# First layer's norm gain moved from the input into the split of the weights, and 39 unread matmuls at the end

## The chip, the cores and the metric

The kernel runs on one core of a Trainium2 chip. The metric is the device time of one execution in microseconds (us); the median of the runs is compared. The engines are TensorE (PE in the profile; its weight loads, PEld, overlap its matmuls), VectorE (DVE), ScalarE (ACT), GpSimd (POOL) and SyncE (SP), which here only issues DMAs. Every engine takes its instructions in the order in which they were written to its queue. A row of a trace gives the start in us, the duration, the engine, the line of the kernel, the operation, out<-in by the program's names, and in square brackets the idle time before it with what ended it.

## The reference

A trunk of four residual layers over 256 tokens of width 1024, float32: pooling mixer, gated DeltaNet, latent attention, pooling mixer again, and a last norm. Each layer adds `mixer(rmsnorm(x, g))` to `x`. What the change touches is the norm and the first product of the first layer:

```python
def rmsnorm(x, g):
    xf = x.astype(jnp.float32)
    y = xf * lax.rsqrt(jnp.mean(xf * xf, axis=-1, keepdims=True) + EPS)
    return (y * g.astype(jnp.float32)).astype(x.dtype)

def pool_mixer(h, w_in, w_grp, scale, w_out):
    B, S, _ = h.shape
    u, gate = jnp.split(h @ w_in, 2, axis=-1)   # w_in: 1024 x 4096
...
    y = p * scale * jax.nn.silu(gate)
    return y @ w_out
```

The DeltaNet layer inverts, for each of 8 heads and 2 chunks of 128 tokens, a unit lower triangle built from keys; the kernel does that by substitution in 32 x 32 blocks and products of blocks.

## The kernel before

Tokens are two tiles of 128 (t = 0, 1), the width is 8 channel tiles of 128 (k). A float32 product is made of three float32r products: both operands are split into a high and a low part (hi, lo) and hi·hi, hi·lo and lo·hi are summed in PSUM.

- *Weights.* `weights()` loads a unit of one or two channel tiles by 512 columns (`raw`, L104, one DMA of SP's queue, 256 or 512 KB), and splits each channel tile: ACT casts it to `whi` (L117), DVE, or POOL for the tiles listed in `pool`, subtracts that from `raw` to get `wlo` (L119). `whi` and `wlo` lie in rings of 9 slots; a `raw` buffer is free for the next load when both have read it. `project()` runs the products token-major (L167, 512 columns of weights) or channel-major (L127 to L129, 256 tokens).
- *The norm.* `part_done` squares and sums a row's part on ACT (L209); POOL makes the mean and its inverse root `xr` (L245 to L251, L296). `Normed.rest` makes h = x * xr * gain, on DVE (L303); where POOL has already made `hg` = x * gain (L291), ACT scales that (L308). `gain` is the layer's vector, broadcast to 128 partitions by two DMAs of 256 KB (L276). `LayerIn.feed` transposes h on PE (L323) and splits it into `hTh` (ACT, L195) and `hTl` (DVE, L200).
- *The start.* 24 transposes of the identity (L270) run on PE while x and the first weights load. SP's queue asks for x of tile 0, then the gains with the first weights between them, then the second tile's x among more weights. Six units of weights of the first product, gate 3 of layer 0, are prefetched as single tiles.
- *The DeltaNet layer* goes through a written list, `g0 k0 d a0 g1 k1 a1 s q0 v0 i v1 v2 q1 g2 u0 v3 u1 g3`: gates (g), keys (k), triangles (a), the substitution (s), queries (q), values (v), inverses (i). Convolutions of queries and values run on DVE (L636, tiles `cv`, `vc`). The substitution stores triangles (L718), loads them as one row of 32 x 32 blocks (`Lb`, L721), runs 31 steps of two operations each on POOL (`pr` L726, `Tb` L730), stores the result (`d_t`, L732) and loads it into `T` by 8 DMAs (L736), on SP's queue. The inverses begin with DVE's transpose U<-T (L797) and PE's products with T (L806).
- *Order.* The code is not run as written: the framework's scheduler, which works with a timeline of its own, puts the instructions of each engine in an order when the kernel is built, and also chooses the number of buffers where the code gives none. So an edit in layer 0 can change the order in other layers. Positions below are taken from the built programs.
- *The end.* `layer_out` adds the last output product to x in parts (L353), the last norm follows, and two DMAs store each tile (L346).

Of the kernel before, what the change touches and what calls it, by code (L numbers as in the profile page):

```python
# [42 lines left out]
def trunk(ctx: ExitStack, tc: tile.TileContext, x, positions, norm_g, pool_w_in, pool_w_grp,  # L43
# [53 lines left out]
    def weights(src, n, cols, raw=None, pool=()):  # L97
        """One unit of weights, split into two float32r parts that add up to it."""
# [11 lines left out]
        for k in range(n):  # L110
# [5 lines left out]
            with later(*(held_back["after"] if held else ())):  # L116
                a = nc.scalar.copy(hi, v)  # L117
                e = nc.gpsimd if k in pool else nc.vector
                b = e.tensor_tensor(out=lo, in0=v, in1=hi.bitcast(F32), op=ALU.subtract)  # L119
# [11 lines left out]
    def project(src, ks, act, cols=CW, chan=False, tail=0, done=None, cuts=1,  # L131
                where="acc", pool=()):
        """act (channel-major, split) times a block of columns; src(k0, n) is its weights.

        ks lists the units (first channel tile, how many), in the order to go through them.
        Token-major: one bank per token tile; channel-major: one bank per two
        channel tiles. The last `tail` units go by token tile and by `cuts` parts of the columns,
        each followed by done(t, part, its bank).
        """
        first, last = ks[0][0], sum(ks[-1]) - 1  # L140

        def unit(k0, n):
            return weights(src(k0, n), n, cols,
                           pool=[a for a in range(n) if (k0 + a) % KD in pool])
# [16 lines left out]
        def rows(t, c, k0, n, parts):  # L161
            o, sl = banks[t][c][:, :width], slice(c * width, (c + 1) * width)
            for x, y in ((0, 0), (0, 1), (1, 0)) if n == 1 else ((0, None), (1, 0)):
                for j in range(n):
                    k = k0 + j
                    for z in (0, 1) if y is None else (y,):
                        nc.tensor.matmul(o, lhsT=act(k, t * P, P)[x], rhs=parts[j][z][:, sl],  # L167
                                         start=k == first and x == z == 0,
                                         stop=k == last and x == 1)
# [21 lines left out]
    def split_out(*tiles):  # L191
        """Tiles of one bank, each (times a per-partition scale) into two float32r parts."""
# [18 lines left out]
    class Split:  # L211
        """Channel-major activations in two float32r parts, four channel tiles to a tile."""
# [20 lines left out]
    # ---- the residual stream. The square sum of a row but its last part goes along with that  # L233
    # part, as the square of one more column ----
# [23 lines left out]
    load_x(0)  # L258
    neghalf = const.tile([P, 2], F32, name="neghalf")
# [5 lines left out]
    # the activation table and TensorE's clock, while the first loads run  # L265
# [3 lines left out]
    for _ in range(WARM):  # L269
        nc.tensor.transpose(ps[:, :P], ident, ident)  # L270

    def gain_tile(row, between):
        g = gp.tile([P, D], F32, tag="gain", name="gain")
        for c in range(2):
            sl = slice(c * CW, (c + 1) * CW)
            nc.sync.dma_start(out=g[:, sl], in_=row[:, sl].to_broadcast([P, CW]))  # L276
            if c == 0 and between:
                between()
        return g

    class Normed:
        """The residual over its mean square's root, times a gain. Every other part of a row
        meets the gain before the root is known."""

        def __init__(self, row, between=None):
            self.g, self.early = gain_tile(row, between), {}
# [7 lines left out]
        def rest(self, t):  # L294
# [17 lines left out]
    class LayerIn(Normed):  # L312
        """The normed residual of a layer, channel-major, made one token tile at a time."""

        def __init__(self, i, between=None):
            super().__init__(norm_g[i:i + 1, :], between)
            self.hT = Split("hT", KD)
# [30 lines left out]
    def layer_out(w, yT, ks, i):  # L348
        """The output projection into the residual, and the start of the next layer."""
# [5 lines left out]

        project(cols_of(w, 0), ks, yT, done=lambda t, c, ps: done(t, 0, ps))
# [41 lines left out]
    def window_counts():  # L398
        """w / (t + 1) for the first tokens of the pooling windows."""
# [10 lines left out]
    # ================= multi-scale causal pooling =================  # L410
    def pool_layer(i, j, hT):
        yT = Split("yT", POOL_W // P)
        order = (3, 2, 1, 0)

        def gate(g):
            ks = [(k, 1) for k in range(KD)] if g == order[0] and i == 0 else units(KD)
            banks = project(cols_of(pool_w_in[j], POOL_W + g * CW), ks, hT, chan=g != order[0])
# [5 lines left out]
        def pooled(g):  # L423
            w = WINDOWS[g]
            banks = project(cols_of(pool_w_in[j], g * CW), units(KD), hT, chan=True)
# [67 lines left out]
    # ================= gated DeltaNet =================  # L493
    GC = {}

    def gdn_setup():
# [16 lines left out]
        # convolution taps, one column per (tap, channel tile)  # L513
# [21 lines left out]
    def gdn_layer(i, j, hT):  # L535
# [27 lines left out]
        # beta and the log decays  # L563
# [38 lines left out]
        # decays: DT[t][j, h, i] = exp(G_i - G_j) for i >= j, and exp(G_i) for the second chunk  # L602
# [25 lines left out]
        def conv(*tiles):  # L628
            """Causal depthwise convolution of the channel tiles of a bank."""
# [10 lines left out]
        # the substitution's unit diagonals, and room for the inverses  # L640
# [18 lines left out]
        def channels(dst, c0, hf, which):  # L659
            """Four heads of keys or queries, channel-major, and their square sums."""  # L660
# [586 lines left out]
```

## Time and profile before

| | us |
|---|---|
| median of 3 runs | 872.19 (870.34 to 872.74) |
| span of the profiled execution | 864.8 |
| PE busy | 843.5 |
| DVE busy | 590.0 |
| ACT busy | 488.1 |
| POOL busy | 156.6 |

The profiled execution's own time is known as its span, from its first to its last instruction on the engines; the median of the runs is 7.4 us above it. In the page the busy time of each engine is a share of the span, the chain that ended last follows the work back from the last instruction to what released it, and the waits say how long an engine stood idle and what ended that. In the view of windows a row gives a stretch, its length, the busy time of PE, PEld, DVE, ACT and POOL with the count of instructions, then the clock that PE was granted (1.00 is full), the share of the DMA engines' time, and GB/s. In a row of groups, the numbers behind the bar are busy time in us, mean duration in ns, and idle time before with what ended it.

### The profile page before, as it was taken

What the parts mean: (1) busy time and instruction counts of PE and PEld (TensorE: products, weight loads), DVE (VectorE), ACT (ScalarE), POOL (GpSimd) and SP (SyncE); (2) the same over time, 40 slices, a digit from 0 to 9 for tenths busy, and PEclk for the clock granted to TensorE, in tenths of its full rate; (3) what the DMA queues carried; (4) which work ended last, traced back from release to release, by engine and by line L of the source; (5) the groups of instructions that cost most, each with busy time, mean ns of one, the idle gap of its engine ahead of it and who ended that gap; (6) DMA issues with size and microseconds to landing.
All of it is one profiled execution on the core that took longest, in us unless ns stands there. A gap on an engine that the chain in (4) does not pass through costs nothing.

```text
span 864.8 us, 16123 instructions
## 1 busy us (share of the span) xinstructions
PE 843.5 (98%) x5965; PEld 779.9 (90%) x5965; DVE 590.0 (68%) x1138; ACT 488.1 (56%) x1007; POOL 156.6 (18%) x290
## 2 busy tenths in 40 slices
PE   7999999999999979999999999999999999999996
PEld 6999998988999868888989989988978989999986
DVE  5588776466889666466567658767766667867852
ACT  5566655468756535455555645555554566565542
POOL 4010000233258932022202002000000110000012
PEclk8999999999999989999999999999999999999999
DMA  6766656557565463123567676632542547566651
GB/s 211 235 194 185 183 172 219 171 158 228 158 172 168 124 191 102 46 84 137 146 183 221 170 171 194 190 104 75 171 146 59 181 144 207 188 180 191 196 194 50
DMA packets 111288, 140.43 MB, mean 162 GB/s; under 512 B 23340, under 2 KB 53224, under 8 KB 111208
## 3 DMA queue, kind: packets, MB, share of 16 engines
q1 hardware_dynamic: 109056, 138.17, 53.4%
q0 software_dynamic: 320, 1.06, 0.4%
q8 instruction: 47, 0.77, 0.4%
q10 hardware_dynamic: 1832, 0.16, 0.2%
q14 instruction: 33, 0.27, 0.1%
HBM read 137.79 MB, written 1.58 MB: 161 GB/s over the span
## 4 chain that ended last, share of the span: by engine, by line
PE 85%; POOL 7%; DVE 3%; DMA 2%; issue 1%; ACT 1%; SPq 1%; POOLq 0%; ACTq 0%; DVEq 0%
PE acc L167 34%; PE acc L128 11%; PE acc L127 11%; PE acc L129 11%; PE aux L127 2%; POOL Tb L730 2%; PE aux L128 2%; POOL pr L726 2%; PE aux L129 2%; DMA gain<-in_norm_g_dram 1%; PE aux L1134 1%; DVE h L303 1%; DVE wlo L119 1%; PE aux L688 1%; PE tp L1159 1%
## 5 line engine op out<-in xcount | busy, mean ns | idle before, releaser
L119 DVE TENSOR_TENSOR wlo<-raw,whi 128x512 fp32r<-128x512 f32 (+1 forms) x491 | 336.9, 709 | 166.6 <-ACT whi L117 160.1
L117 ACT CAST whi<-raw 128x512 fp32r<-128x512 f32 (+1 forms) x508 | 301.4, 617 | 262.8 <-PE acc L167 92.3
L127 PE MATMUL acc<-hTh,whi 128*128 128x256 f32 x832 | 235.8, 284 | 3.3 <-DVE cv L636 3.3
L128 PE MATMUL acc<-hTl,whi 128*128 128x256 f32 x832 | 236.1, 284 | 0.0
L129 PE MATMUL acc<-hTh,wlo 128*128 128x256 f32 x832 | 235.4, 283 | 0.0
L127 PEld LDWEIGHTS acc<-hTh,whi 128*128 128x128 f32 x832 | 158.2, 190 | 4.2 <-ACT whi L117 3.7
L128 PEld LDWEIGHTS acc<-hTl,whi 128*128 128x128 f32 x832 | 158.3, 190 | 0.4
L129 PEld LDWEIGHTS acc<-hTh,wlo 128*128 128x128 f32 x832 | 158.3, 190 | 0.2
L167 PE MATMUL acc<-whi,yTh 128*128 128x256 f32 (+1 forms) x384 | 116.3, 323 | 0.0
L167 PE MATMUL acc<-wlo,yTh 128*128 128x256 f32 (+1 forms) x384 | 116.2, 319 | 0.0
L167 PE MATMUL acc<-whi,yTl 128*128 128x256 f32 (+1 forms) x384 | 92.4, 321 | 0.0
L167 PEld LDWEIGHTS acc<-whi,yTh 128*128 128x128 f32 x384 | 71.9, 188 | 5.2
L167 PEld LDWEIGHTS acc<-wlo,yTh 128*128 128x128 f32 x384 | 72.0, 188 | 5.1
L167 PEld LDWEIGHTS acc<-whi,yTl 128*128 128x128 f32 x384 | 63.1, 188 | 5.6
L291 POOL TENSOR_TENSOR hg<-x,gain 128x256 f32<-128x256 f32 x18 | 15.4, 860 | 271.7 <-DVE x L353 267.9
L167 PE MATMUL acc<-wlo,hTh 128*128 128x512 f32 (+1 forms) x144 | 56.5, 396 | 0.8 <-DVE wlo L119 0.5
L167 PE MATMUL acc<-whi,hTh 128*128 128x512 f32 (+1 forms) x144 | 55.9, 394 | 0.7 <-ACT hTh L195 0.7
L167 PE MATMUL acc<-whi,hTl 128*128 128x512 f32 (+1 forms) x144 | 45.8, 390 | 0.0
L434 POOL COPY win<-u 128x4 f32<-128x4 f32 x8 | 2.8, 353 | 176.8 <-ACT u L428 176.8
L167 PEld LDWEIGHTS acc<-wlo,hTh 128*128 128x128 f32 x144 | 27.4, 191 | 7.6 <-DVE wlo L119 2.1
L167 PEld LDWEIGHTS acc<-whi,hTh 128*128 128x128 f32 x144 | 27.5, 191 | 6.6 <-ACT hTh L195 1.4
L119 POOL TENSOR_TENSOR wlo<-raw,whi 128x512 fp32r<-128x512 f32 x17 | 23.6, 1389 | 49.4 <-ACT whi L117 49.3
(336 smaller groups left out, 1440.8 us busy)
## 6 DMA issues: line engine op xcount, KB each, us to landing
raw<-in_pool_w_in_dram SPq DMA_DIRECT2D x60, 512.0 KB, 4.5
raw<-in_gdn_w_in_dram SPq DMA_DIRECT2D x48, 512.0 KB, 3.9
raw<-in_pool_w_out_dram SPq DMA_DIRECT2D x32, 512.0 KB, 3.9
raw<-in_mla_w_in_dram SPq DMA_DIRECT2D x24, 512.0 KB, 4.4
raw<-in_mla_w_uq_dram SPq DMA_DIRECT2D x36, 256.0 KB, 3.4
raw<-in_pool_w_grp_dram SPq DMA_DIRECT2D x16, 512.0 KB, 4.0
raw<-in_gdn_w_out_dram SPq DMA_DIRECT2D x16, 512.0 KB, 3.7
raw<-in_mla_w_ukv_dram SPq DMA_DIRECT2D x32, 256.0 KB, 3.2
```

The source lines that it names most:

```text
L117: a = nc.scalar.copy(hi, v)
L119: b = e.tensor_tensor(out=lo, in0=v, in1=hi.bitcast(F32), op=ALU.subtract)
L127: nc.tensor.matmul(o, lhsT=lhs[0], rhs=rhs[0], start=start, stop=False)
L128: nc.tensor.matmul(o, lhsT=lhs[0], rhs=rhs[1], start=False, stop=False)
L129: nc.tensor.matmul(o, lhsT=lhs[1], rhs=rhs[0], start=False, stop=stop)
L167: nc.tensor.matmul(o, lhsT=act(k, t * P, P)[x], rhs=parts[j][z][:, sl], start=k == first and x == z == 0, stop=k == last and x == 1)
L291: nc.gpsimd.tensor_tensor(out=self.early[t, a], in0=xs[t][:, sl], in1=self.g[:, sl], op=ALU.mult)
L303: nc.vector.scalar_tensor_tensor(out=h[:, cut:], in0=xs[t][:, sl], scalar=r[:, 0:1], in1=self.g[:, sl], op0=ALU.mult, op1=ALU.mult)
L688: nc.tensor.matmul(ps[:, b], lhsT=kT[hf][:, b, tt], rhs=rhs[hf][:, b, tt], start=True, stop=True)
L726: nc.gpsimd.tensor_tensor(out=pv, op=ALU.mult, in0=Lb[:, r, r + 1:, None].to_broadcast([M * Q, n, c]), in1=Tb[:, r:r + 1, :c].to_broadcast ...
L730: nc.gpsimd.tensor_tensor(out=tv, in0=tv, in1=pv, op=ALU.subtract)
L1134: nc.tensor.matmul(ps[:, spans[0]], lhsT=r0[bb, pr], rhs=krT[bb], start=False, stop=False)
```

## The change

Layer 0 no longer multiplies its input by the gain; the gain of channel tile k scales the rows of the weights of that tile while they are split. For this the 1024 gains are loaded as 8 rows of 128 (4 KB, ACT's queue, L269 of the changed kernel), transposed on PE in the middle of the 24 warm-up transposes and copied to `gain0`, one column per channel tile (DVE). In the split, ACT's cast becomes an activation with a scale, and the subtraction a scalar_tensor_tensor (raw * gain - whi), always on DVE. h of layer 0 is x * xr, one tensor_scalar. The two broadcast DMAs of layer 0, POOL's two `hg` and its one `wlo` of layer 0 go. Behind the last product 39 matmuls follow, whose results nobody reads. Other layers are computed as before. Comments and docstrings are dropped, which is left out here.

```diff
-    def weights(src, n, cols, raw=None, pool=()):
+    def weights(src, n, cols, raw=None, pool=(), gains=None):
...
-                a = nc.scalar.copy(hi, v)
-                e = nc.gpsimd if k in pool else nc.vector
-                b = e.tensor_tensor(out=lo, in0=v, in1=hi.bitcast(F32), op=ALU.subtract)
+                if gains is not None:
+                    a = nc.scalar.activation(hi, v, AF.Copy, scale=gains[:, k:k + 1])
+                    b = nc.vector.scalar_tensor_tensor(out=lo, in0=v, scalar=gains[:, k:k + 1],
+                                                       in1=hi.bitcast(F32), op0=ALU.mult,
+                                                       op1=ALU.subtract)
+                else:
+                    a = nc.scalar.copy(hi, v)
+                    e = nc.gpsimd if k in pool else nc.vector
+                    b = e.tensor_tensor(out=lo, in0=v, in1=hi.bitcast(F32), op=ALU.subtract)
...
     load_x(0)
+    grow = const.tile([KD, P], F32, name="grow0")
+    nc.scalar.dma_start(out=grow, in_=norm_g[0].rearrange("(k p) -> k p", p=P))
...
-    for _ in range(WARM):
-        nc.tensor.transpose(ps[:, :P], ident, ident)
+    for n in range(WARM):
+        last = nc.tensor.transpose(ps[:, :P], ident, ident)
+        if n == WARM // 2:
+            with later(last.ins):
+                pg = bank(tps, "tp")
+                last = nc.tensor.transpose(pg[:, :KD], grow, ident[:KD, :KD])
+            gain0 = const.tile([P, KD], F32, name="gain0")
+            nc.vector.tensor_copy(gain0, pg[:, :KD])
...
                 h = wh.tile([P, CW], F32, tag="h", name="h")
+                if self.g is None:
+                    nc.vector.tensor_scalar(h, xs[t][:, a:a + CW], r[:, 0:1], None, ALU.mult)
+                    hs.append(h)
+                    continue
...
-            super().__init__(norm_g[i:i + 1, :], between)
+            super().__init__(norm_g[i:i + 1, :] if i else None)
...
-    def prefetch(k, pool=()):
-        ready.append(weights(first(k, 1), 1, CW, worka("raw", CW), pool))
+    def prefetch(k):
+        ready.append(weights(first(k, 1), 1, CW, worka("raw", CW), gains=gain0[:, k:k + 1]))
...
-            for a in range(0, D, CW):
-                if t:
-                    nxt.begin(t, a)
             nxt.feed(t)
...
-    nxt = LayerIn(0, lambda: prefetch(0, (0,)))
-    for k in range(1, E0):
+    nxt = LayerIn(0)
+    for k in range(E0):
         prefetch(k)
...
+    y = held_back["y"]
+    lhs, (b0, b1) = y(0, 0, P)[0], (y.part(x)[0] for x in (1, 2))
+    f16, whole = MC["mask16"], ident
+    with later(held_back["pe"]):
+        ps = bank(tps, "tp")
+        flat = b0.rearrange("p k s -> p (k s)")
+        for n, w, v, out_ in (
+                (6, lhs, b0[:, 1], ps[:, :S]),
+                (6, MC["ident16"], f16, ps[:, :P]),
+                (6, lhs, b0[:, 1, :P], ps[:, :P]),
+                (6, lhs, flat[:, :2 * S:2], ps[:, :S]),
+                (6, lhs, b1[:, 0:2, :P], ps[:, :S].rearrange("p (a s) -> p a s", a=2)),
+                (5, lhs, flat[:, :CW], ps),
+                (4, whole, whole, ps[:, :P])):
+            for _ in range(n):
+                nc.tensor.matmul(out_, lhsT=w, rhs=v, start=True, stop=True)
```

The order of instructions moves with it at the start, and in the DeltaNet layer. The lines of the changed kernel are some 8 to 23 higher: L256, L104, L276 become L265, L105, L293; L303 becomes L317, L119 L120 (with gains) or L126, L200 L209; L726, L730, L732, L736 become L749, L753, L755, L759, and L806 L829.

SP's queue at the start, before (x_93 and x_94 are the two tiles of x):

```order
L256 DMA x_93<-in_x_dram 128x512 x2
L276 DMA gain<-in_norm_g_dram 128x512
L104 DMA raw<-in_pool_w_in_dram 128x512
L276 DMA gain<-in_norm_g_dram 128x512
L104 DMA raw<-in_pool_w_in_dram 128x512 x3
L256 DMA x_94<-in_x_dram 128x512
L104 DMA raw<-in_pool_w_in_dram 128x512
L256 DMA x_94<-in_x_dram 128x512
L104 DMA raw<-in_pool_w_in_dram 128x512 x3
```

and now:

```order
L265 DMA x_93<-in_x_dram 128x512 x2
L105 DMA raw<-in_pool_w_in_dram 128x512 x4
L265 DMA x_94<-in_x_dram 128x512 x2
L105 DMA raw<-in_pool_w_in_dram 128x512 x2
L105 DMA raw<-in_pool_w_in_dram 128x2x512
L105 DMA raw<-in_pool_w_in_dram 128x512 x2
L105 DMA raw<-in_pool_w_in_dram 128x2x512 x11
```

The gains are gone, x of the second tile comes earlier, and two single units of weights (channel tiles 4 and 5) now stand behind two others and a double unit. DVE's queue at the start, before:

```order
L303 SCALAR_TENSOR_TENSOR h<-x_93,xr,gain 128x512 x2
L119 TENSOR_TENSOR wlo<-raw,whi 128x512
L200 TENSOR_TENSOR hTl_169<-tp,hTh_168 128x4x128
L200 TENSOR_TENSOR hTl_178<-tp,hTh_177 128x4x128
L119 TENSOR_TENSOR wlo<-raw,whi 128x512 x4
L303 SCALAR_TENSOR_TENSOR h<-x_94,xr,gain 128x256 x2
L119 TENSOR_TENSOR wlo<-raw,whi 128x512 x2
```

and now:

```order
L317 TENSOR_SCALAR h<-x_93,xr 128x512 x2
L287 COPY gain_126<-tp 128x8
L120 SCALAR_TENSOR_TENSOR wlo<-raw,gain_126,whi 128x512 x2
L209 TENSOR_TENSOR hTl_172<-tp,hTh_171 128x4x128
L209 TENSOR_TENSOR hTl_181<-tp,hTh_180 128x4x128
L120 SCALAR_TENSOR_TENSOR wlo<-raw,gain_126,whi 128x512 x3
L317 TENSOR_SCALAR h<-x_94,xr 128x512 x2
L120 SCALAR_TENSOR_TENSOR wlo<-raw,gain_126,whi 128x512 x3
L399 MEMSET rows 128x128
L424 CAST cnt<-cnti 128x16
L120 SCALAR_TENSOR_TENSOR wlo<-raw,gain_126,whi 128x512
L209 TENSOR_TENSOR hTl_172<-tp,hTh_171 128x4x128
```

The wlo that was POOL's is DVE's, and h of the second tile is made whole on DVE. POOL's queue in the last third of the substitution, before (the sizes, 240 down to 31, tell the steps):

```order
L730 TENSOR_TENSOR Tb<-Tb,pr 64x12x20
L119 TENSOR_TENSOR wlo<-raw,whi 128x512
L726 TENSOR_TENSOR pr<-Lb,Tb 64x231
L730 TENSOR_TENSOR Tb<-Tb,pr 64x11x21
L726 TENSOR_TENSOR pr<-Lb,Tb 64x220
L730 TENSOR_TENSOR Tb<-Tb,pr 64x10x22
L726 TENSOR_TENSOR pr<-Lb,Tb 64x207
L730 TENSOR_TENSOR Tb<-Tb,pr 64x9x23
L726 TENSOR_TENSOR pr<-Lb,Tb 64x192
L119 TENSOR_TENSOR wlo<-raw,whi 128x512
L730 TENSOR_TENSOR Tb<-Tb,pr 64x8x24
```

and now:

```order
L126 TENSOR_TENSOR wlo<-raw,whi 128x512
L749 TENSOR_TENSOR pr<-Lb,Tb 64x135
L753 TENSOR_TENSOR Tb<-Tb,pr 64x5x27
L749 TENSOR_TENSOR pr<-Lb,Tb 64x112
L753 TENSOR_TENSOR Tb<-Tb,pr 64x4x28
L749 TENSOR_TENSOR pr<-Lb,Tb 64x87
L753 TENSOR_TENSOR Tb<-Tb,pr 64x3x29
L749 TENSOR_TENSOR pr<-Lb,Tb 64x60
L753 TENSOR_TENSOR Tb<-Tb,pr 64x2x30
L749 TENSOR_TENSOR pr<-Lb,Tb 64x31
L126 TENSOR_TENSOR wlo<-raw,whi 128x512
L753 TENSOR_TENSOR Tb<-Tb,pr 64x31
```

The two wlo, both of gate 2 (its channel tiles 3 and 7), stand later in the chain, the second just before its last operation. SP's queue behind it, before:

```order
L104 DMA raw<-in_gdn_w_in_dram 128x2x512 x15
L732 DMA d_t<-Tb 64x1024
L104 DMA raw<-in_gdn_w_in_dram 128x2x512
L736 DMA T<-d_t 32x8x32 x8
L104 DMA raw<-in_gdn_w_in_dram 128x2x512 x2
```

and now:

```order
L105 DMA raw<-in_gdn_w_in_dram 128x2x512 x13
L755 DMA d_t<-Tb 64x1024
L759 DMA T<-d_t 32x8x32
L105 DMA raw<-in_gdn_w_in_dram 128x2x512
L759 DMA T<-d_t 32x8x32 x4
L105 DMA raw<-in_gdn_w_in_dram 128x2x512
L759 DMA T<-d_t 32x8x32 x3
L105 DMA raw<-in_gdn_w_in_dram 128x2x512 x3
```

Two loads of weights that stood ahead of `d_t` or right behind it now stand among the loads of `T`. On PE, 42 products (L127 to L129) of the last values stand between gate 2 and the first product with T (L806) before; now 16 stand there, and the other 26 behind it.

More of the change, by code (lines that the diff above doesn't have):

```diff
@@ L131, in project @@
     def project(src, ks, act, cols=CW, chan=False, tail=0, done=None, cuts=1,
-                where="acc", pool=()):
+                where="acc", pool=(), gains=None):
         first, last = ks[0][0], sum(ks[-1]) - 1
@@ L143, in unit @@
             return weights(src(k0, n), n, cols,
-                           pool=[a for a in range(n) if (k0 + a) % KD in pool])
+                           pool=[a for a in range(n) if (k0 + a) % KD in pool],
+                           gains=None if gains is None else gains[:, k0:k0 + n])
         if chan:
@@ L166, in rows @@
                     for z in (0, 1) if y is None else (y,):
-                        nc.tensor.matmul(o, lhsT=act(k, t * P, P)[x], rhs=parts[j][z][:, sl],
-                                         start=k == first and x == z == 0,
-                                         stop=k == last and x == 1)
+                        m = nc.tensor.matmul(o, lhsT=act(k, t * P, P)[x], rhs=parts[j][z][:, sl],
+                                             start=k == first and x == z == 0,
+                                             stop=k == last and x == 1)
+            held_back["pe"] = m.ins
         held = []
@@ L276, in gain_tile, with __init__ @@
             nc.sync.dma_start(out=g[:, sl], in_=row[:, sl].to_broadcast([P, CW]))
-            if c == 0 and between:
-                between()
         return g
     class Normed:
-        def __init__(self, row, between=None):
-            self.g, self.early = gain_tile(row, between), {}
+        def __init__(self, row):
+            self.g, self.early = None if row is None else gain_tile(row), {}
         def begin(self, t, a):
```

11 lines of the change are left out of this document (7 added, 4 removed).

## The prediction

> **What bounds the kernel now.** I read the page's busy shares first, then the chain that ended last, then the idle time of PE by what ended it, and only then the timeline of those places.
>
> ```profile
> span 864.8 us, 16123 instructions
> PE 843.5 (98%) x5965; PEld 779.9 (90%) x5965; DVE 590.0 (68%) x1138; ACT 488.1 (56%) x1007; POOL 156.6 (18%) x290
> ...
> PE 85%; POOL 7%; DVE 3%; DMA 2%; issue 1%; ACT 1%; SPq 1%; POOLq 0%; ACTq 0%; DVEq 0%
> ...
> PE tp L323 <- DVE h L303: 4.3, 2, 2.7
> PE acc L127 <- DVE cv L636: 3.3, 1, 3.3
> PE aux L806 <- DMA T<-d_t: 2.6, 1, 2.6
> ```
>
> PE works 843.5 of 864.8 us. The waits of PE name all that is left: two at the start for the normed input h (4.3 us together), two in the DeltaNet layer (3.3 for the convolution, 2.6 for T, the inverse blocks that come back from DRAM), and little else. So no edit beside running PE work can gain; only the first 12 us, the DeltaNet's substitution, the tail behind PE, and the number of PE instructions can move the time. The share of POOL (7%) in the chain is that substitution.
>
> **The head.** What PE waits for at the start is the chain up to the first product.
>
> ```profile
> 5.36 0.57 POOL L296 TENSOR_TENSOR xr<-ms,neghalf 128x1 f32<-128x1 f32 x1
> 8.14 0.75 DVE L303 SCALAR_TENSOR_TENSOR h<-x,xr,gain 128x512 f32<-128x512 f32 x1 [8.14 <-DMA gain<-in_norm_g_dram]
> 9.82 1.27 POOL L119 TENSOR_TENSOR wlo<-raw,whi 128x512 fp32r<-128x512 f32 x1 [3.89 <-ACT whi L117]
> 9.87 1.77 DVE L303 SCALAR_TENSOR_TENSOR h<-x,xr,gain 128x512 f32<-128x512 f32 x1 [0.97 <-DMA gain<-in_norm_g_dram]
> 11.00 0.58 ACT L195 CAST hTh<-tp 128x512 fp32r<-128x512 f32 x1
> 12.45 0.78 PE L167 MATMUL acc<-whi,hTh 128*128 128x512 f32 x1
> ...
> 2.65 7.12 DMA gain<-in_norm_g_dram
> ...
> 16.12 1.65 ACT L117 CAST whi<-raw 128x512 fp32r<-128x512 f32 x3
> 18.16 1.47 DVE L119 TENSOR_TENSOR wlo<-raw,whi 128x512 fp32r<-128x512 f32 x2
> 20.32 0.68 DVE L200 TENSOR_TENSOR hTl<-tp,hTh 128x512 fp32r<-128x512 f32 x1
> ...
> 14.00:16.00 2.00, 2.00 (x7) 1.54 (x6) 2.00 (x4) 2.00 (x5) 1.24 (x2) 0.58 0.78 291
> ```
>
> The root xr is there at 5.36 + 0.57 = 5.93, but h waits until 8.14 and 9.87 for the two broadcast gains, the second of which took 7.12 us to land. The change drops both transfers for this layer: h is then x times xr, and can start at about 5.95. From there I walk the new order with spacings of these rows: ACT 0.55 an operation (three in 1.65), DVE 0.65. Two h end at 7.3; the copy of the transposed gains, 128x8, follows (nearest 0.2, like the small DVE rows of this kernel), 7.5; two whi, 8.6; hTh, 0.58, 9.2. If the new h, which reads one tensor less, is a little quicker, it is 8.7. So the first product starts at about **8.7 to 9.2 instead of 12.45**.
>
> That is not all kept. After it, DVE has, up to the low part hTl of the second token tile, 2 hTl, 9 wlo, 2 more h and a few small ones: 7.5 + 13 x 0.65 + 0.3 + 0.7 = 16.9, with one wait for ACT's hTh at the start about 17.2; before, that instruction ended at 20.32 + 0.68 = 21.0. PE itself took 21.0 - 12.45 = 8.6 us from its first product to there, with the clock at a mean of 0.58 still from 14 to 16. With the same slow start it is there at 9.0 + 8.6 = 17.6; at full clock it is a good microsecond earlier, but then DVE holds it at 17.2. Both say **-3.5**; from there on PE has the same products, without idle time. Bounds: -4.3, all of the 4.3 of idle time; -2.5, if the unread part of the walk (4 KB of gains by ACT's queue, two raw units that go behind 1 MB of others because two buffers fewer are used) costs one more microsecond. The gains stand first in ACT's queue, so they are asked for within the first microsecond; even at the broadcast's 7.12 us they land at 8.1, 0.6 later than needed.
>
> **Prices in the split.** Per 128x512 unit the cast becomes an ACTIVATE with a scale, and the subtraction a scalar_tensor_tensor, on 64 units of layer 0.
>
> ```profile
> L443 DVE SCALAR_TENSOR_TENSOR p<-win,u 128x1024 f32<-128x1024 f32 x4 | 4.9, 1214 | 0.0
> L446 DVE TENSOR_TENSOR pl<-p,ph 128x1024 fp32r<-128x1024 f32 x4 | 4.9, 1215 | 0.0
> ...
> L774 ACT ACTIVATE vc<-vc 128x512 f32<-128x512 f32 x8 | 5.1, 633 | 3.7 <-DVE vc L636 3.7
> L117 ACT CAST whi<-raw 128x512 fp32r<-128x512 f32 x500 | 297.9, 620 | 260.1 <-PE acc L167 91.4 <-PE acc L128 77.2 <-DMA raw<-in_gdn_w_in_dram 30.9
> ...
> 50.00:75.00 25.00, 25.00 (x190) 23.91 (x190) 22.30 (x38) 16.15 (x29) 2.00 (x3) 1.00 0.68 194
> ```
>
> On DVE the two forms cost the same (1214 and 1215 ns at twice the width). On ACT it is 633 against 620: 64 x 13 ns = 0.8 us, in a layer where ACT is busy 16.15 of 25 us and waits for PE to free its ring. So **0**; if that cover were gone, +0.8. One wlo and two hg leave POOL, and land in the DVE count above.
>
> **The DeltaNet layer.** The diff doesn't touch it, yet the order there changes, and the wait for T is there.
>
> ```profile
> 260.22 0.23 POOL L726 TENSOR_TENSOR pr<-Lb,Tb 64x31 f32<-64x31 f32 x1 [1.51 <-DMA Lb<-d_l]
> 277.79 1.04 POOL L730 TENSOR_TENSOR Tb<-Tb,pr 64x240 f32<-64x240 f32 x1
> 293.14 0.69 POOL L730 TENSOR_TENSOR Tb<-Tb,pr 64x240 f32<-64x240 f32 x1
> 293.80 1.28 POOL L119 TENSOR_TENSOR wlo<-raw,whi 128x512 fp32r<-128x512 f32 x1
> 299.47 1.29 POOL L119 TENSOR_TENSOR wlo<-raw,whi 128x512 fp32r<-128x512 f32 x1
> 310.60 0.25 POOL L730 TENSOR_TENSOR Tb<-Tb,pr 64x31 f32<-64x31 f32 x1
> ...
> 310.87 0.46 SPq L732 DMA_DIRECT2D d_t<-Tb  x1
> 311.42 0.54 SPq L104 DMA_DIRECT2D raw<-in_gdn_w_in_dram  x1
> ...
> 306.44 0.55 PE L127 MATMUL acc<-hTh,whi 128*128 128x256 f32 x1 [3.28 <-DVE cv L636]
> 312.84 0.28 PE L127 MATMUL acc<-hTh,whi 128*128 128x256 f32 x1
> 313.89 0.28 PE L127 MATMUL acc<-hTh,whi 128*128 128x256 f32 x1
> 317.04 1.97 PE L806 MATMUL aux<-T,LT 128*128 128x64 f32 x16 [2.63 <-DMA T<-d_t]
> ...
> 293.80:299.50 5.70, 5.70 (x26) 4.49 (x25) 0.00 (x0) 0.54 (x2) 5.23 (x10) 1.00 0.53 174
> 299.50:311.00 11.50, 8.22 (x37) 7.07 (x36) 10.80 (x19) 4.64 (x10) 10.40 (x18) 0.77 0.47 142
> 308.00:310.00 2.00, 2.00 (x12) 2.00 (x11) 2.00 (x5) 1.13 (x2) 1.77 (x4) 0.50 0.68 175
> 317.03:352.30 35.27, 34.47 (x271) 30.89 (x272) 22.34 (x38) 17.53 (x38) 5.31 (x6) 1.00 0.44 136
> ```
>
> POOL sets T: its chain runs from 260.22 to 310.85 without a break, and T is read 6.2 us later. Its start hangs on PE's products before, so it moves with the head. Three things differ behind that.
>
> First, work for PE while it waits. Before, 42 products of the values stand ahead of the matmul on T (L806); now 16. A product takes (313.89 - 312.84) / 9 = 0.117 us, so 26 x 0.117 = 3.0 us moves from a stretch where PE waited anyway to one where it is busy 34.47 of 35.27 us: **+3.0** in full.
>
> Second, when T comes. The two wlo that gate 2 needs from POOL stood at 293.80 and 299.47; now they stand five steps and one step before the end of the chain. What they cost in the chain is unchanged (1.28 + 1.29), but gate 2, the raw loads and with them DVE stand still for longer meanwhile. While DVE did nothing (293.80:299.50, 0.00 busy) POOL's steps took their short time; the same 64x240 step took 1.04 at 277.79 and 0.69 at 293.14. The 11.5 us from 299.50 to 311.00, with DVE 10.80 busy, hold 18 operations; the steps there are smaller, so I give each about half of that 0.35: 18 x 0.16 = 2.9, up to -2.9. Against it, the transfers of T have two raw loads of 512 KB among them, where one stood before (0.54 of the queue each, and their bytes): +0.5 to +1.5. I take -0.7, from -2 to +1.
>
> Third, what PE meets behind T: a clock that may have dropped (after the gap of 3.28 it ran at 0.50 from 306 on; the gap of 2.63 left it at 1.00), and values whose weights were fetched later. At half clock a product takes twice its 0.117; 16 of them are +1.9. A late weight costs at most another wait like half of the 2.63, +1.3. From 0 to 3.2 together; I take 0.5, nearer to nothing, as 35 us of other PE work lie there to fill in. By the Trainium skill, "TensorE: Matmul & The Clock Gate", section "Part 1: The HAM clock gate (the "warmup" mystery)", the clock drops to half after an idle window of about 3.4 us; the two gaps here lie on either side of a limit near 3, and if the gap ahead of T is longer than that, the rule would add 1.9 in the place of 0.5 and give 873.4. The sum for the layer is 3.0 - 0.7 + 0.5 = **+2.8**, from +0.5 to +5.5.
>
> What would the Trainium skill make of POOL's speed? In "SBUF — State Buffer", section "Who interferes with whom", VectorE's second pair of ports is GpSimd's only one, under an exclusive lock. The trace agrees (1.77 against 0.75 for the h that ran beside POOL's wlo, 0.69 against 1.04 for the step above). By that rule, with DVE standing still, the second point is the full -2.9, which is the first rival.
>
> **Layers 2 and 3 and the tail.** MLA and the last pool layer get other orders too, but the waits above name none of PE's there. A new one might be half as long as the longest of those above, 0 to +1.5; I take +0.3. Behind the last product 39 unread matmuls follow.
>
> ```profile
> 857.59 0.39 PE L167 MATMUL acc<-whi,yTl 128*128 128x256 f32 x2
> 859.94 0.91 ACT L308 ACTIVATE h<-hg,xr 128x256 f32<-128x256 f32 x2 [0.66 <-POOL xr L296]
> ```
>
> PE ends at 857.98, the span at 864.8: 6.8 us of norm and store cover them. At 0.117 for 256 columns and twice that for 512, with the whole float32 and strided ones up to three times as long, I estimate 5.1 to 7.2 us for them: 0 to +0.4, **+0.2**. Nothing reads them; if they were ahead of the last product they would cost all of it.
>
> The sum: -3.5 + 0 + 2.8 + 0.3 + 0.2 = **-0.2**. The profiled execution has only its span, 864.8; the median of the runs, 872.19, is 7.4 above it, and I carry that over: **872.0**.
>
> **Rivals.** (a) *Faster*: the head is kept and the substitution ends early, because DVE stands still. For it: the short steps at 293.80:299.50. Against: gate 2 and the raws that stand still too must be made up behind T. The layer then costs 3.0 - 2.9 + 0.5 = 0.6, and the sum is -3.5 + 0.6 + 0.3 + 0.2 = -2.4; with the head at its bound of -4.3 it is -3.2, 869.0, and with no new wait behind T 868.5. (b) *Slower*: PE is starved around T. The second wlo is one step before the end of the chain and waits for its whi, whose raw waits for earlier wlo of that chain; if this raw lands late, POOL itself stands, T comes later, and PE, with 16 products instead of 42, falls to half clock. For it: ACT waits 30.9 us for these raws in all, and the clock's drop at 306. It decides from about 2 us of standing: 2.8 + 2.7 - 3.5 + 0.5 = +2.5 or more, 875 to 877. (c) *The head isn't kept*: PE starts at 9 but DVE and ACT, fed by late raws, bring it to the same point at 19.5 instead of 17.5: -1.5 + 2.8 + 0.5 = +1.8, 874.
>
> **How the numbers follow.** My case 0.40, (a) 0.25, (b) 0.20, (c) 0.15. A measurement of this kernel can tell about 0.3%, 2.6 us: 869.6 to 874.8 is no change. My case lies within it but for a tenth; (a) is faster in most of it; (b) slower; (c) within, a third slower. That makes faster 0.28, same 0.47, slower 0.25. The range holds my case, (c), and the near part of both others: 867.5 to 876.5.
>
> **What would show it.** The first L175 product at about 9 and no wait for a gain; hTl of the second tile ending at about 17.3; the first d_l store some 3.5 earlier; the chain on POOL ending near 306 (307 without the gain); L829 on T with more than 2.6 us of idle time ahead of it; the stretch behind it about 38 us long where it was 35.3; PE's last unread matmul before the last store lands. I am wrong if PE has new idle time in MLA or the last layer, which no row before hints at, or if the moved products find a gap behind T to lie in.

## The result, and the profile after

| | before | changed |
|---|---|---|
| median, us | 871.29 (870.34 to 872.74, 4 runs) | 883.40 (880.83 to 884.12, 4 runs) |
| ratio, 95% interval | | 1.0144 (1.0117 to 1.0170) |
| span of the profiled execution | 864.8 | 882.3 |

The change makes the kernel 12.1 us slower, well above the forecast of 872.0 and above its range. In every execution whose span is known the time is 1.7 to 1.8 above the span. So the profiled execution of before took about 866.5, not 872: the prediction took most of an ordinary spread between runs (864.9 to 873.5 in the comparisons below) for time around the span. For the same reason the two traces lie 17.5 us apart, 5 more than the medians. The trace still tells where, but its differences are about 5 us too large in all.

The page after, with the idle time of PE by what ended it:

```profile
span 882.3 us, 16222 instructions
PE 856.2 (97%) x6009; PEld 785.6 (89%) x6009; DVE 596.4 (68%) x1140; ACT 493.7 (56%) x1005; POOL 153.5 (17%) x287
...
PE acc L134 <- DVE vc L659: 4.9, 1, 4.9
PE aux L829 <- DMA T<-d_t: 4.3, 1, 4.3
PE acc L175 <- ACT hTh L204: 2.0, 4, 0.8
PE aux L892 <- ACT gsg L579: 1.7, 1, 1.7
PE tp L938 <- DVE yg L929: 1.6, 1, 1.6
PE acc L175 <- DVE wlo L126: 1.6, 2, 0.9
PE acc L175 <- ACT whi L119: 1.5, 1, 1.5
```

The waits for h are gone from the list, as forecast. But others are new or longer, most of them in the DeltaNet layer: 4.9 for `vc`, a convolution on DVE, 4.3 for T instead of 2.6, and 1.7 and 1.6 in the part behind the inverses, where before had none. The last addition to x in each layer shows how the difference grows. First of before, layers 0 to 3, then of the changed kernel:

```profile
174.41 0.41 DVE L353 TENSOR_TENSOR x<-acc,x 128x256 f32<-128x256 f32 x1
427.26 0.41 DVE L353 TENSOR_TENSOR x<-acc,x 128x256 f32<-128x256 f32 x1
696.01 0.42 DVE L353 TENSOR_TENSOR x<-acc,x 128x256 f32<-128x256 f32 x1 [0.17 <-PE acc L167]
858.02 0.42 DVE L353 TENSOR_TENSOR x<-acc,x 128x256 f32<-128x256 f32 x1 [1.27 <-PE acc L167]
```

```profile
173.02 0.41 DVE L373 TENSOR_TENSOR x<-acc,x 128x256 f32<-128x256 f32 x1
442.18 0.41 DVE L373 TENSOR_TENSOR x<-acc,x 128x256 f32<-128x256 f32 x1
712.80 0.41 DVE L373 TENSOR_TENSOR x<-acc,x 128x256 f32<-128x256 f32 x1
875.43 0.42 DVE L373 TENSOR_TENSOR x<-acc,x 128x256 f32<-128x256 f32 x1 [1.27 <-PE acc L175]
```

The differences are -1.4, +14.9, +16.8 and +17.4. Layer 0 wins 1.4 instead of 3.5, the DeltaNet layer loses 16.3, latent attention 1.9, the last layer 0.6, and behind the last addition nothing changes (6.8 and 6.9 us to the end).

The built programs differ in one more thing that the diff doesn't name, and that I had not looked at. Neither kernel writes down how many buffers the PSUM pools and the pool of work tiles get; the framework searches for them. Before, it had settled on 6 banks (buffers in PSUM that products are summed in) at most in use for the projections (`acc`), 4 for the smaller products (`aux`) and 6 work tiles; for the changed kernel its search stopped at 4, 2 and 4. All experiments below start from this.

### The profile page after: what moved, and what is told of

It is laid out like the page before. It is cut to its first block, busy times and chain, and to the rows that moved or that the text cites. A ratio compares the mean times of both kernels' runs of the same rounds, so it can differ in the third digit from the quotient of the medians.

```text
span 882.3 us, 16222 instructions
## 1 busy us (share of the span) xinstructions
PE 856.2 (97%) x6009; PEld 785.6 (89%) x6009; DVE 596.4 (68%) x1140; ACT 493.7 (56%) x1005; POOL 153.5 (17%) x287
## 4 chain that ended last, share of the span: by engine, by line
PE 64%; POOL 7%; DMA 3%; DVE 3%; ACT 2%; issue 2%; SPq 0%; ACTq 0%; POOLq 0%; DVEq 0%
PE acc L175 25%; PE acc L135 8%; PE acc L136 8%; PE acc L134 8%; POOL pr L749 2%; POOL Tb L753 2%; PE aux L134 2%; DVE wlo L126 1%; PE aux L136 1%; PE aux L135 1%; DMA raw<-in_gdn_w_in_dram 1%; PE aux L1157 1%; PE tp L1253 1%; PE aux L711 1%; PE aux L829 1%
## 5 line engine op out<-in xcount | busy, mean ns | idle before, releaser
L124 ACT CAST whi<-raw 128x512 fp32r<-128x512 f32 (+1 forms) x444 | 263.9, 617 | 239.9 <-PE acc L175 93.8
L126 DVE TENSOR_TENSOR wlo<-raw,whi 128x512 fp32r<-128x512 f32 (+1 forms) x428 | 296.1, 714 | 150.4 <-ACT whi L124 147.2
L175 PE MATMUL acc<-whi,yTh 128*128 128x256 f32 (+1 forms) x384 | 114.4, 324 | 1.0 <-ACT yTh L206 0.8
L175 PE MATMUL acc<-whi,yTl 128*128 128x256 f32 (+1 forms) x384 | 89.9, 319 | 0.0
L306 POOL TENSOR_TENSOR hg<-x,gain 128x256 f32<-128x256 f32 x16 | 13.6, 852 | 268.5 <-DVE x L373 266.5
L119 ACT ACTIVATE whi<-raw,gain 128x512 fp32r<-128x512 f32 x64 | 43.9, 721 | 28.6 <-DMA raw<-in_pool_w_in_dram 16.7
L120 DVE SCALAR_TENSOR_TENSOR wlo<-raw,gain,whi 128x512 fp32r<-128x512 f32 x64 | 46.2, 747 | 14.7 <-ACT whi L119 13.3
```

The lines of the kernel that those rows point to most:

```text
L119: a = nc.scalar.activation(hi, v, AF.Copy, scale=gains[:, k:k + 1])
L120: b = nc.vector.scalar_tensor_tensor(out=lo, in0=v, scalar=gains[:, k:k + 1], in1=hi.bitcast(F32), op0=ALU.mult, op1=ALU.subtract)
L175: m = nc.tensor.matmul(o, lhsT=act(k, t * P, P)[x], rhs=parts[j][z][:, sl], start=k == first and x == z == 0, stop=k == last and x == 1)
L306: nc.gpsimd.tensor_tensor(out=self.early[t, a], in0=xs[t][:, sl], in1=self.g[:, sl], op=ALU.mult)
```

## The experiments

Theory A says that the loss comes from these counts. Theory B says that it comes from the edit's own instructions and their order. Each run is compared with runs of the kernel before on the same chip. The chips differ (before took 870.05 to 871.10), so two experiments are compared by their ratios.

| run | what | us | before | ratio (95%) |
|---|---|---|---|---|
| e1 | changed, acc 6, aux 4 | 867.53 | 870.05 | 0.9980 (0.9960 to 1.0001) |
| e2 | e1, work tiles 6 | 870.69 | 870.05 | 1.0015 (0.9998 to 1.0032) |
| e3 | before, acc 4, aux 2, work 4 | 884.23 | 870.05 | 1.0182 (1.0141 to 1.0223) |
| e4 | changed, no unread matmuls | 882.27 | 870.05 | 1.0157 (1.0123 to 1.0190) |
| e5 | before, work 4 | 869.72 | 871.10 | 0.9983 (0.9970 to 0.9997) |
| e6 | before, acc 4 | 874.38 | 871.10 | 1.0041 (1.0026 to 1.0056) |
| e7 | before, aux 2 | 880.72 | 871.10 | 1.0119 (1.0086 to 1.0152) |
| e8 | e1, POOL free of gate 2 | 868.72 | 871.10 | 0.9973 (0.9962 to 0.9984) |
| e9 | e1, plain cast | 867.62 | 871.10 | 0.9967 (0.9946 to 0.9987) |
| e10 | e2, plain cast | 867.62 | 871.10 | 0.9961 (0.9940 to 0.9982) |
| e11 | e10, POOL free of gate 2 | 865.59 | 871.10 | 0.9943 (0.9925 to 0.9962) |
| e12 | before, POOL free of gate 2 | 869.48 | 870.78 | 0.9992 (0.9974 to 1.0010) |

### e1 and e3: the counts given to the changed kernel, and taken from the one before

```diff
-    acc = ctx.enter_context(tc.tile_pool(name="acc", space=PSUM))
-    aux = ctx.enter_context(tc.tile_pool(name="aux", space=PSUM))
+    acc = ctx.enter_context(tc.tile_pool(name="acc", bufs=6, space=PSUM))
+    aux = ctx.enter_context(tc.tile_pool(name="aux", bufs=4, space=PSUM))
```

> The changed kernel with the PSUM pools' buffers written down as the kernel before has them: acc 6, aux 4 (the changed kernel was built with acc 4, aux 2). Theory A, the banks: the 16 us lost in the DeltaNet layer come from the fewer banks; without that loss the time is about 868 to 872 us, with the head's gain of about 1.4 left, PE waits for T under 3 us and none over 1 us behind the inverses. Theory B, the split: dearer activations (721 ns against 617) and the new order hold engines up in themselves; then the time stays at 881 to 884.

e3 is the kernel before with `bufs` 4 for `acc`, 2 for `aux` and 4 for the work tiles:

> The kernel before, nothing of the change in it, built with acc 4, aux 2 and 4 work buffers, as the changed kernel was. Theory A: 881 to 886 us, slower by 10 to 15, with the loss between the DeltaNet layer's start and its end. Theory B: within 2 us of before.

867.53 and 884.23: theory A in both directions. With the banks of before, the changed kernel loses nothing; with the changed kernel's counts, the kernel before loses 14.2 us without a line of the edit. The last additions tell the same. e3 ends its layers at 173.79, 441.63, 712.80 and 875.43, within 0.8 of the changed kernel each time. The end of the DeltaNet layer in e3, then in e1:

```profile
441.63 0.41 DVE L353 TENSOR_TENSOR x<-acc,x 128x256 f32<-128x256 f32 x1
428.63 0.41 DVE L373 TENSOR_TENSOR x<-acc,x 128x256 f32<-128x256 f32 x1
```

The counts also decide the order. In e2 and e10 below, which have all three counts of before, PE's instructions of the DeltaNet layer come in the order of before. So the order that theory B speaks of comes with the counts and not with the edit. How much of the loss is waiting for banks, and how much is the order that fewer of them bring, the runs don't tell. Three waits of PE in e3:

```profile
PE acc L127 <- DVE vc L636: 4.7, 1, 4.7
PE aux L812 <- DVE X L808: 4.1, 1, 4.1
PE tp L323 <- DVE h L303: 2.8, 2, 2.2
```

The wait for `vc` is the one of the changed kernel (4.9), in a kernel that has the old split. Two details of e1's expectation failed: PE waits 7.2 us for T there, not under 3, and the head's gain is 0.7 and not 1.4. The long wait for T did not make e1 slow: its DeltaNet layer ends 1.4 later than in the trace of before, where the changed kernel's ends 14.9 later.

### e6, e7 and e5: one count at a time

```diff
-    acc = ctx.enter_context(tc.tile_pool(name="acc", space=PSUM))
+    acc = ctx.enter_context(tc.tile_pool(name="acc", bufs=4, space=PSUM))
```

The other counts are written down as before has them. e7 has `acc` 6 and `aux` 2, e5 both banks as before and 4 work tiles.

> The kernel before with only the banks of the projections cut from 6 to 4. If the projections' banks carry the loss (PE can't begin the next product before DVE has read the last one: the wait for vc, 4.9 us near 268 in the changed kernel), 6 to 12 us slower and that wait is there; if the aux banks carry it, within 4 us and no such wait.

> The kernel before with only the aux banks cut from 4 to 2. These hold the products of inverses and of the two chunks. If they carry the loss, 6 to 12 us slower, with new waits of PE from 317 on and from 360 to 400, where the changed kernel lost 9; if the projections' banks do, within 4 us.

> The kernel before with only its work tiles cut from 6 buffers to 4 (banks as they were). Theory A1, the PSUM banks carry the loss: within 3 us of before, as the work tiles changed the time by 3 between the two runs with banks given. Theory A2, the work tiles carry it (convolutions and the first raws live in them): 6 to 12 us slower.

Fewer `acc` banks cost 3.3 us, fewer `aux` banks 9.6, fewer work tiles nothing (1.4 faster). 3.3 + 9.6 - 1.4 = 11.5 of the 14.2 in e3 add up; the rest is less than the spread of e7's four runs (877.8 to 883.8). The waits, first of e6, then of e7:

```profile
PE acc L127 <- DVE vc L636: 4.2, 1, 4.2
PE tp L323 <- DVE h L303: 3.9, 2, 2.2
PE acc L127 <- DVE cv L636: 3.5, 2, 2.7
```

```profile
PE tp L323 <- DVE h L303: 3.8, 2, 1.9
PE tp L323 <- ACT h L308: 3.7, 1, 3.7
PE acc L127 <- DVE cv L636: 3.3, 1, 3.3
PE aux L806 <- DMA T<-d_t: 2.5, 1, 2.5
```

In e6 PE waits for `vc` near 268, as in the changed kernel: the convolution on DVE reads `acc`, and PE's next product needs a bank of it. But that wait isn't where e6 loses: T is read at 312.62 there, 4.4 earlier than before, and the layer still ends 6.3 later, at 433.59. In e7 the wait for `vc` is missing, and T comes as before. There the loss comes later, in short waits of the two chunks and of attention, and 3.7 us at the start of the last layer. My two guesses for these runs were too clean: each pool costs something, and `aux` the most, but not only where the changed kernel had lost it. In the trace of the DeltaNet layer neither run stands out: it takes 259.4 us in e6 and 258.5 in e7, and in e2 and e10, with all counts and PE's order as before, 258.6 and 259.8. Only with both pools small does it take 267.8 (e3) and 269.2 (the changed kernel).

### e4: the unread matmuls

The block behind the last product is left out, so 39 matmuls fewer run, whose results nobody reads.

> The changed kernel without the 39 unread matmuls behind the last product. If they are hidden under the last norm and the stores, as forecast: within 0.5 us of the changed kernel, 882 to 884. If they cost what PE takes for them: 877 to 878.

882.27 against 883.40: inside the spread of either (880.8 to 884.1), and against before the ratios are 1.0157 and 1.0144, so hidden or nearly. In the changed kernel they begin when PE is done:

```profile
875.23 0.88 PE L1253 MATMUL tp<-yTh,yTh 128*128 128x256 f32 x6
875.95 0.51 PE L1253 MATMUL tp<-mask,ident 128*128 128x128 bf16 x6
876.27 4.18 PE L1253 MATMUL tp<-yTh,yTh 128*128 128x128 f32 x23
880.28 1.06 PE L1253 MATMUL tp<-ident 128*128 128x128 f32 x8
```

They end at 881.34, 6.0 us after the last product and 1.0 before the end of the span. The last store is issued at 878.36 and its kind lands within 2.3 us, so by 880.7: the unread matmuls outlast it by 0.7, but from the last addition to the end of the span it is 6.9 us with them (882.3 - 875.43) and 6.8 without (879.7 - 872.93 in e4). The build without them got the same counts, 4, 2 and 4, and the same order of PE in the DeltaNet layer: they are not what changed the search.

### e2, e9 and e10: where the rest of the head went

The head gave 1.4 us and e1 kept 0.7 of it, where 3.5 were forecast. Its rows in the changed kernel:

```profile
8.96 0.50 PE L175 MATMUL acc<-whi,hTh 128*128 128x512 f32 x1 [0.78 <-ACT hTh L204]
13.39 3.22 ACT L119 ACTIVATE whi<-raw,gain 128x512 fp32r<-128x512 f32 x5 [1.39 <-DMA raw<-in_pool_w_in_dram]
14.16 0.50 PE L175 MATMUL acc<-whi,hTh 128*128 128x512 f32 x1 [1.55 <-ACT whi L119]
18.95 1.27 DVE L209 TENSOR_TENSOR hTl<-tp,hTh 128x512 fp32r<-128x512 f32 x2
...
L119 ACT ACTIVATE whi<-raw,gain 128x512 fp32r<-128x512 f32 x64 | 43.9, 721 | 28.6 <-DMA raw<-in_pool_w_in_dram 16.7 <-PE acc L135 4.9 <-PE aux L135 2.3
L120 DVE SCALAR_TENSOR_TENSOR wlo<-raw,gain,whi 128x512 fp32r<-128x512 f32 x64 | 46.2, 747 | 14.7 <-ACT whi L119 13.3 <-PE acc L136 1.3
```

The first product starts at 8.96, in the forecast stretch. Then two things go wrong. Channel tile 4 comes late (ACT waits 1.39, PE 1.55), the two raw units behind 1 MB of others; and ACT's scaled activation takes 721 ns instead of 620. e2 gives the work tiles back (`bufs=6`), so that the raws find a slot early. e9 and e10 take the scale out of ACT:

```diff
-                    a = nc.scalar.activation(hi, v, AF.Copy, scale=gains[:, k:k + 1])
+                    a = nc.scalar.copy(hi, v)
```

The high part is then that of the unscaled weight, and the low part, w * gain - hi, takes the rest, so both still add up to w * gain.

> As the run before, and the pool of work tiles that holds the first six raw units also as before (6 buffers, where the changed kernel has 4). Theory A with the late raw: channel tiles 4 and 5 need not wait for DVE to free a slot, so PE's gap of 1.55 us near 12.6 goes and gate 3 ends 2 to 3.5 us earlier than before instead of 1.3; 867 to 871 us in all. If the late raw is not what the head lost, gate 3 ends 1.3 earlier as in the changed kernel. Theory B: 881 to 884.

> The first run's kernel (banks given, 4 work tiles) with ACT's scaled activation put back to a plain cast: hi = cast(w), lo = w * gain - hi, which still add up to w * gain. It measures the dearer activation (721 ns against 617 to 620) by itself: 64 of them, and the wait of the first for the gains. If ACT's price is hidden in layer 0, within 1 us of the first run (866.5 to 868.5); if ACT feeds PE late at the head, 1 to 2 us less, with gate 3 earlier by as much and a shorter gap near 12.5.

> The second run's kernel (banks given, 6 work tiles) with the plain cast. Here the raws of tiles 4 and 5 come early, so what is left of the head is ACT and the second tile's h. If ACT's operations hold the head, the store of the triangles comes 1 to 2 us earlier than in the second run, and with 42 products ahead of T as before the time is 868 to 869.5; if not, 870 to 871 as the second run.

The end of layer 0 against before (174.41) in the traces: changed -1.4, e1 -0.7, e2 -1.9, e9 -2.0, e10 -3.3. So each remedy gives 1.3 on top of the other, and both together nearly the forecast head. Alone, each seems to give 1.3 over e1 too, but against the changed kernel only 0.6, and part of the difference is the clock: in e1 PE ran at half clock for a stretch of the head, and in the changed kernel, e2 and e9 it did not (1.00 from 8 to 20):

```profile
14.60:18.01 3.41, 3.28 (x12) 2.88 (x13) 3.41 (x6) 2.38 (x4) 2.83 (x27) 0.50 0.01 2
```

These are single traces. In the five runs of the kernel before that leave layer 0's code alone (e3, e5, e6, e7, e12), the layer ends between 173.14 and 174.83. ACT's group in e9 is the evidence for the price:

```profile
L119 ACT CAST whi<-raw 128x512 fp32r<-128x512 f32 x64 | 37.7, 619 | 28.7 <-DMA raw<-in_pool_w_in_dram 16.6 <-PE acc L135 5.4 <-PE aux L135 2.7
```

In time it shows less. e9 is not clearly faster than e1 (0.9967 and 0.9980), and e10 (0.9961) is faster than e2 (1.0015) but not than e9. The wait for T is longer with the plain cast (7.7 for 7.2, and 3.9 for 3.3), so it takes back a part of what the head wins.

### e8, e11 and e12: POOL free for the substitution

```diff
-                            pool=((0, 4), (7,), (3, 7), (7,))[vi])
+                            pool=((0, 4), (7,), (), (7,))[vi])
```

> The changed kernel with banks given as in the first run (acc 6, aux 4), and both wlo of gate 2 on DVE, so that POOL has nothing but the substitution after 262. In the first run PE waited 7.2 us for T, and these two took 1.27 and 1.29 of POOL's chain. If the chain sets T, T comes 2 to 2.6 us earlier and the time is 865 to 866; if what lies behind T absorbs it, or DVE, which takes two more, slows POOL as much, 867 to 868.

> As the run before, and both wlo of gate 2 on DVE, as in the fourth run with the change. If T's chain and the head add up: 866 to 867.5; if PE only waits longer for T and then runs at half clock, as there (9.4 us of waiting), 868 to 870.

> The kernel before, banks and work tiles as it has them, with both wlo of gate 2 on DVE and nothing of the change. It tells how much of the fastest run's 5.5 us (865.6 against 871.1) comes from the change's head. If the head carries it (gate 3 ended 3.6 earlier there): within 1.5 us of before, 869.5 to 872. If POOL's chain carries it: 866 to 868.

e8 alone brings nothing that can be told over e1 (0.9973 and 0.9980), and 868.72 is a little above both halves of its expectation. POOL's chain is 2.3 us shorter than in e1 (48.3 for 50.5), but begins 1.4 later, so T is read only 0.8 earlier; PE waits 9.4 us for it. With the whole head, e11 is the fastest of all, 865.59, below both halves of its expectation, 5.5 us faster than before and some 17 faster than the change as it was made. e12 shows no gain of POOL's part alone that can be told from none (0.9992, from 0.9974 to 1.0010, so at most 2.3 us). Two rows and two windows of e11:

```profile
170.87 0.41 DVE L373 TENSOR_TENSOR x<-acc,x 128x256 f32<-128x256 f32 x1
311.35 3.65 PE L829 MATMUL aux<-T,LT 128*128 128x64 f32 x16 [9.76 <-DMA T<-d_t]
...
314.00:318.00 4.00, 4.00 (x20) 4.00 (x20) 2.98 (x4) 0.62 (x1) 0.00 (x0) 0.50 0.90 311
318.00:320.00 2.00, 2.00 (x20) 2.00 (x18) 0.00 (x0) 1.62 (x5) 0.00 (x0) 0.99 0.33 126
```

Layer 0 ends 3.5 earlier than before, T is read at 311.35 instead of 317.04, and PE stands still for 9.76 us ahead of it; behind that it works at half clock, and the 16 products with T take 3.65 instead of 1.97. Whether a kernel gains by giving PE something to do in that gap was not tried.

## Why the prediction was wrong, by its own steps

- *What bounds the kernel*: right that PE is the bound, wrong that only the places named could move. The loss came behind T and in the layers after it, where PE had hardly waited before. The error was to take the buffers as given, although the bound of the head speaks of "two buffers fewer": that the work tiles had lost two was seen, and the banks were not looked up.
- *The head, -3.5*: the mechanism was right, the size not. It gave -1.4. Mis-sized were the late raw units, for which the bound of -2.5 allowed one microsecond (PE's gap alone was 1.55), and ACT's price. With both mended, e10 and e11 measure -3.3 and -3.5, each in one trace. The forecast took PE's clock at the start to make no difference ("Both say -3.5"). In e1, which gives PE the same order in the head as the changed kernel, layer 0 ended 0.7 later than there, with the stretch at half clock shown above.
- *Prices in the split, 0*: the row was the wrong one. `vc<-vc` (633 ns) has no scale per partition. The trace of before had a nearer one: `h<-hg,xr` scales by a column, and takes 503 ns at half the width, against 417 of a square without:

```profile
L308 ACT ACTIVATE h<-hg,xr 128x256 f32<-128x256 f32 x18 | 8.2, 503 | 3.3 <-POOL xr L296 3.3
...
L209 ACT ACTIVATE junk<-x 128x256 f32<-128x256 f32 x8 | 3.3, 417 | 10.1 <-DVE x L353 10.1
```

  These 86 ns more are near the 101 that were measured (721 - 620), though the second row is another function. The Trainium skill has it too: "ScalarE: Activation LUTs", section "What ACT_TABLE_LOAD costs", gives about 93 ns for each operand that points to one value per partition, and the traces agree. On DVE the scaled form takes 747 ns where the plain one takes 689, also not the forecast nothing. In the middle of layer 0 both are hidden, as forecast (from 28 to 173 PE waits for nothing in either trace); at its start ACT feeds PE, and they are not.
- *The DeltaNet layer, +2.8 (0.5 to 5.5)*: **this step failed**. It measured +16.3 in the traces; as e2 and e10 take 258.6 and 259.8 us in PE's order of before, where the trace of before has 252.9, some 6 or 7 of it can be chance, and 9 to 16 is what the fewer banks cost here. I read the order of the queues around T, saw that 26 products and two wlo had moved, and priced these moves by themselves. They were symptoms of the smaller counts, and I put what else they bring behind T at 0.5. The stretch from the first product with T to the end of the layer, first before, then changed:

```profile
317.04:427.26 110.22, 109.37 (x721) 97.78 (x722) 67.05 (x128) 59.07 (x147) 22.93 (x49) 1.00 0.35 112
```

```profile
318.67:442.18 123.51, 119.29 (x752) 104.18 (x752) 73.62 (x140) 62.70 (x155) 22.74 (x49) 0.96 0.34 107
```

  It is 13.3 us longer. By these rows and the 0.117 us of a product I estimate 3.6 for 31 more instructions of PE (the moved products, forecast at 3.0), 4.9 for the clock of 0.96, and 3.4 for idle time (4.2 where before has 0.9): new waits in the two chunks. For the clock and the waits behind T together the forecast had 0.5. The wait of 4.9 us for `vc`, near 268, stands ahead of T, which POOL's chain sets; it costs at most the 1.6 by which T came later than before.

  That T came later was misread too. The forecast (-3.5 for the head, -2 to +1 for the chain) had it 2.5 to 5.5 earlier, and the first store of the triangles 3.5 earlier; the store came 0.2 later (249.78 for 249.57). The chain on POOL was shorter, as forecast (49.4 us for 50.6), but from its end to the first product with T it took 9.3 us instead of 6.2, where 0.5 to 1.5 had been put down for the two loads of weights among those of T. A long wait for T need not harm: e1 waits 7.2 us there and is still as fast as before.
- *Layers 2 and 3, +0.3*: +2.5 in the trace, above the bound of 1.5. The counts carry this too: from the end of the DeltaNet layer to the last addition it is 430.8 us before and 430.5 in e1, 433.3 in the changed kernel and 433.8 in e3.
- *The tail, +0.2*: right (6.8 and 6.9 us from the last addition to the end). The unread matmuls took 6.1 us, where 5.1 to 7.2 was estimated, but did not end before the last store landed.
- *The rivals*: the third, that the head isn't kept, came true in part, for the reason given there. The second named the right layer and sign, and PE did run at half clock behind T (from 317.8 to 324.6), but a late raw on POOL's chain is not what happened. The first, faster, did not come. No rival had the banks.
- *Time around the span*: 1.7 and not 7.4, see above. As the sum was carried over to the median, the forecast is not moved by it, only the reason given for the 7.4 was wrong.

Open is why the search for buffers stopped early. The unread matmuls aren't the reason (e4). The changed start is what is left, but no run shows it, and which line of it was not tried.

## What to carry to other kernels

Where a framework chooses buffer counts, compare what both builds got before pricing an edit, and write the counts down: here an edit at the first 10 us cost 12 us, most of it in another layer, because of numbers that no line of the diff contains. When an order changes far from the edit, ask for the resource behind it before pricing the moves. And price an instruction by a row with the same kinds of operands: a scale from a column of SBUF isn't a scale that stands in the instruction.

## What the runs showed of the hardware

PE's clock can fall without a long gap. In the changed kernel it fell at 375.9, with no gap over 1.63 us in the 3.5 us before it:

```profile
369.50:372.40 2.90, 2.90 (x14) 2.30 (x13) 1.10 (x3) 1.23 (x5) 0.00 (x0) 1.00 0.00 0
372.40:375.90 3.50, 1.79 (x8) 1.20 (x8) 1.50 (x4) 0.74 (x3) 1.35 (x4) 0.99 0.01 2
375.90:379.30 3.40, 3.38 (x11) 2.19 (x10) 0.67 (x2) 1.68 (x6) 0.85 (x3) 0.50 0.00 0
379.30:382.00 2.70, 2.70 (x14) 2.21 (x13) 1.91 (x5) 0.04 (x1) 0.49 (x2) 1.00 0.00 0
```

PE was busy for 1.79 of the 3.5 us ahead, and then ran at half clock for 3.4 although it was busy all the time. In the prediction a limit near 3 us between the gaps of 2.63 and 3.28 seemed to decide; this row shows that it doesn't. How full such a stretch is doesn't decide alone either. Before (the first two rows) and in e10 (the last two) PE was busy for nearly the same share, with the same longest gap of 0.8, and the clock stayed up before and fell in e10:

```profile
350.19:353.61 3.42, 2.63 (x31) 2.46 (x30) 1.63 (x3) 0.00 (x0) 0.00 (x0) 1.00 0.49 153
353.61:357.00 3.39, 3.39 (x20) 3.06 (x19) 1.91 (x8) 1.88 (x6) 0.00 (x0) 1.00 0.00 0
348.30:351.70 3.40, 2.61 (x20) 2.11 (x19) 1.99 (x3) 1.14 (x2) 0.00 (x0) 0.98 0.12 33
351.70:355.00 3.30, 3.30 (x23) 3.18 (x24) 0.68 (x1) 0.00 (x0) 0.00 (x0) 0.50 0.34 125
```

What does decide, these runs don't show. "TensorE: Matmul & The Clock Gate" of the Trainium skill, section "Part 1: The HAM clock gate (the "warmup" mystery)", speaks of a free-running window of 3413 ns and of an idle one; the length agrees (half clock for 3.4 us here, and for 6.8 from 317.8), but a window that was half busy was enough here.
